# Storing the split feed-forward weights right after their split, ahead of a later weight's load

## The chip, the cores and the metric

The kernel runs on one core of a Trainium2 chip. A core has five engines with a queue of instructions each: TensorE (PE in the profile, its weight loads PEld), VectorE (DVE), ScalarE (ACT), GpSimd (POOL) and SyncE (SP), which computes nothing here and issues nearly all DMAs. Every queue is worked off in its order: an instruction that waits holds up those behind it. The metric is the device time of one execution in microseconds (us), and less is better.

## The reference

One transformer block of an encoder, in float32, over 2048 tokens of 1024 features: an RMSNorm, a projection into two kinds of attention heads, both attentions, an output projection with a residual, and then the feed-forward part, which the change concerns:

```
u2 = rms_norm(h, norm2_w[l])
gate = jnp.einsum('bsd,df->bsf', u2, w_gate[l])
up = jnp.einsum('bsd,df->bsf', u2, w_up[l])
h = h + jnp.einsum('bsf,fd->bsd', jax.nn.silu(gate) * up, w_down[l])
```

`w_gate` and `w_up` are 1024 x 2816, `w_down` is 2816 x 1024. The same weights serve all 2048 tokens.

## The kernel before

The attention part takes the first half of the execution. The feed-forward part then goes over the tokens in two halves of 1024 tokens. Within a half it goes over 11 groups of 256 hidden features (`NFG`); a group has three weight blocks of 1 MB in float32, for gate (g), up (u) and down (d).

A float32 product is done as three float16 products: every operand is split into a high part (the value rounded to float16) and a low part (what is left). In addition the 2 x 2 block products go by a scheme with seven products in place of eight (`quad` for gate and up, `down`), so each weight block is turned into seven operands of 512 columns, some of them sums and differences of quarters of the block. The seven operands in two parts are one tile `w16` of 128 x 7 x 2 x 512 float16, 1.75 MB. In the profile it is called `wg`, `wu` or `wd`.

In the first half (half 0) `load_ffn` makes this tile from the weight:

- `stage` (L829) issues the load of the block from HBM into one of two places of the tile `stages` (L826), in turn. A load can therefore only go out when the weight two places earlier has been read for the last time.
- ACT squares the block (`sq`, L869, for down L184), PE and DVE find its largest value and from it a power of two as scale (L877, L178, L195 to L199).
- `split_weight` (L207) makes the high part on ACT (L210) and the low part on DVE (L215), operand by operand. POOL makes the sums and differences in place in `stages` (L98), so the later operands wait for POOL. The last low part for the block is the last reader of its place in `stages`.
- A list `keep` takes the finished tile (L918) for a store into the HBM tensor `split`.

In the second half (half 1) nothing is split: `load_ffn` loads `split` back (L860).

The store from `keep` is not issued where it is put on the list. When `stage` has issued the load of a later weight and the list has more than one entry, it issues the oldest entry, tied behind that load by `issue_after` (L835 to L837). In the steady state that is the store of the weight two places earlier. What is left goes out after the last weight (L919 to L921).

The order of the weights is g, d, u, g, d, u and so on: the loop over the groups (L1157) begins the next group's gate in the middle of this group's gate product, this group's down weight in the middle of the down product, and the next group's up in the middle of the up product (`in_gate`, `in_down`, `in_up`, L1177 to L1191). `begin` runs the part of `load_ffn` ahead of its `yield` (load and square), `end` the rest (scale and split). The down product is done for two groups at a time, so the work repeats every two groups.

The order of each engine's queue is written when the kernel is built. A planner goes through the program with its own estimate of when each operand is ready, and puts on an engine's queue what it reckons ready, by priority, which follows the order of the program. `issue_after` adds an edge that the planner must keep. On the chip these queues are fixed, with semaphores for the operands.

Of the kernel before, what the change touches and what calls it, by code (L numbers as in the profile page):

```python
# [21 lines left out]
S, D, P = 2048, 1024, 128  # L22
NT, KT, NC = S // P, D // P, S // 512
FF = 2816
NFG = FF // 256
# [34 lines left out]
def block(tc, a, out):  # L60
    nc = tc.nc
    PE, ACT, DVE, POOL, SP = nc.tensor, nc.scalar, nc.vector, nc.gpsimd, nc.sync
    top = ExitStack()
    with top:
# [8 lines left out]
        def note(e, ns):  # L73
            load[e] += ns * KW[e]
# [34 lines left out]
        def nm(s):  # L109
            uid[0] += 1  # L110
            return f"{s}{uid[0]}"

        def c1(n=1, name="c"):
            t = cp.tile([P, n], F32, name=nm(name))
            return t
# [13 lines left out]
        def times(o, a_, b_, c=None):  # L129
            DVE.tensor_scalar(o[:], a_[:], b_[:], c, op0=ALU.mult, **({} if c is None else {"op1": ALU.mult}))  # L130
# [34 lines left out]
        split = dr.tile([NFG, 3, P, 7 * 2 * 512], F16, name="split")  # L165
# [14 lines left out]
        def scale_begin(pieces, junk=None):  # L180
            m0 = sm.tile([P, 4], F32, tag="m0", name=nm("m0"))
            for j, pc in enumerate(pieces):
                if junk is not None:
                    ACT.activation(junk, pc, AF.Square, accum_out=m0[:, j : j + 1])  # L184
                    note("A", 0.84 * int(np.prod(pc.shape[1:])) + 200)
                else:
                    DVE.tensor_reduce(m0[:, j : j + 1], pc, op=ALU.max, axis=AX.XY if len(pc.shape) > 2 else AX.X, apply_absolute_value=True)
                    note("D", 1.05 * int(np.prod(pc.shape[1:])) + 100)
            return [m0[:, j : j + 1] for j in range(len(pieces))]
# [613 lines left out]
        with ExitStack() as ph2:  # L803
# [12 lines left out]
            def pst(t):  # L816
                pst_n[0] += 1
                if pst_n[0] % 4:
                    return ps2.tile([P, 512], F32, tag="b", bufs=6, name=nm(t))
                return psj.tile([P, 512], F32, tag="pj", name=nm(t))  # L820
# [1 line left out]
            r_2, p_2, r_24 = rp2  # L822
            scales = {}

            keep, rows = [], []
            stages = fw.tile([P, 2, 2048], F32, name="stages", bufs=1)  # L826
            turn = [0]

            def stage(fg, nme):  # L829
                st = stages[:, turn[0]]  # L830
                turn[0] ^= 1
                f0 = 256 * fg
                with tc.issue_after(rows[1].ins) if (fg, nme) == (1, "u") else nullcontext():
                    d = fetch(st, f0, nme)
                if len(keep) > 1:  # L835
                    with tc.issue_after(d.ins):
                        SP.dma_start(*keep.pop(0))  # L837
                return st

            def fetch(st, f0, nme):  # L840
                if nme == "d":
                    return SP.dma_start(st.rearrange("p (f n) -> p f n", f=2), a["w_down"][0, f0 : f0 + 256, :].rearrange("(f p) n -> p f n", p=P))
                return SP.dma_start(st.rearrange("p (k n) -> p k n", k=KT), a["w_gate" if nme == "g" else "w_up"][0, :, f0 : f0 + 256].rearrange("(k p) n -> p k n", p=P))

            ones = fw.tile([P, P], BF16, name="ones", bufs=1)
            DVE.memset(ones[:], 1.0)
# [5 lines left out]
            def load_ffn(half, fg, names, W):  # L852
                eng = "ADP" if fg == 0 else WE
                sc = scales.setdefault(fg, {})
                for nme in names:
                    if half == 1:
                        yield
                        late = nme == "d" and fg == NFG - 1
                        w16 = (fd if nme == "d" and not late else fw).tile([P, 7, 2, 512], F16, tag="wd" if nme == "d" and not late else "wgu", bufs=2, name=nm("w" + nme))
                        SP.dma_start(w16[:].rearrange("p o s n -> p (o s n)"), split[fg, "gud".index(nme)])  # L860
                        W[nme] = w16
                        continue
                    st = stage(fg, nme)
                    r, p, sW = c1(), c1(), c1()
                    sq = fw.tile([P, 2048], BF16, tag="sq", bufs=1, name=nm("sq"))
                    if nme == "d":
                        cols = scale_begin([st], sq[:])
                    else:
                        ACT.activation(sq[:], st, AF.Square)  # L869
                        note("A", 1900)  # L870
                    yield
                    w16 = (fd if nme == "d" else fw).tile([P, 7, 2, 512], F16, tag="wd" if nme == "d" else "wgu", bufs=2, name=nm("w" + nme))
                    pt = pst("fsc")

                    def columns(m):
                        for k in range(KT):
                            PE.matmul(pt[:, :256], lhsT=ones[:], rhs=sq[:, 256 * k : 256 * k + 256], start=k == 0, stop=k == KT - 1)  # L877
                        DVE.tensor_reduce(m, pt[:, :256], op=ALU.max, axis=AX.X)

                    scale_end((lambda m: across(m, pt, cols)) if nme == "d" else columns, r[:], p[:], True, sW)  # L880
                    sc[nme] = (r, p, sW)
                    sW = sc[nme][2]
                    tte = "DP" if fg == 0 else "P"
                    sx = fw.tile([P, 512], F32, tag="sx", bufs=1, name=nm("sx"))

                    def put(o, src, n):
                        split_weight(w16[:, o : o + n, 0], w16[:, o : o + n, 1], src, 512 * n, sW, eng)

                    if nme == "d":
                        sv = st.rearrange("p (f h n) -> p h f n", f=2, h=2)  # L890
                        b11, b21, b12, b22 = sv[:, 0, 0], sv[:, 0, 1], sv[:, 1, 0], sv[:, 1, 1]
                        put(0, sv[:, 0], 2)
                        tt(sx[:], b22, b12, ALU.subtract, 512, tte)
                        tt(b12, b12, b11, ALU.subtract, 512, tte)
                        tt(b11, b22, b12, ALU.subtract, 512, tte)
                        tt(b21, b21, b11, ALU.subtract, 512, tte)
                        put(2, sv[:, 1], 2)
                        put(4, sv[:, 0], 2)
                        put(6, sx[:].unsqueeze(1), 1)
                    else:  # L900
                        sv = st.rearrange("p (d k f n) -> p d k f n", d=2, k=4, f=2)
                        xv = sx[:].rearrange("p (k n) -> p k n", k=4)
                        wv = w16[:].rearrange("p o s (k n) -> p o s k n", k=4)

                        def putk(o, src, n):
                            split_weight(wv[:, o : o + n, 0], wv[:, o : o + n, 1], src, 512 * n, sW, eng)

                        blk = lambda f, d: sv[:, d, :, f, :]
                        putk(0, sv[:, :, :, 0, :], 2)
                        tt(xv, blk(0, 0), blk(1, 0), ALU.subtract, 512, tte)  # L910
                        tt(blk(1, 0), blk(1, 0), blk(1, 1), ALU.add, 512, tte)
                        tt(blk(0, 0), blk(1, 0), blk(0, 0), ALU.subtract, 512, tte)
                        tt(blk(0, 1), blk(0, 1), blk(0, 0), ALU.subtract, 512, tte)
                        putk(2, sv[:, :, :, 1, :], 2)
                        putk(4, sv[:, :, :, 0, :], 2)
                        putk(6, xv.unsqueeze(1), 1)
                    W[nme] = w16
                    keep.append((split[fg, "gud".index(nme)], w16[:].rearrange("p o s n -> p (o s n)")))  # L918
                    if fg == NFG - 1 and nme == "d":  # L919
                        while keep:  # L920
                            SP.dma_start(*keep.pop(0))  # L921
                if half == 0 and "g" in names:
                    kg, F = c1(), c1()
                    times(kg, sc["g"][1], p_2, 2.0 ** -14)
                    times(F, sc["g"][0], r_2, 2.0 ** (21 - 37))
                    sc["kg"], sc["F"] = kg, F
                if half == 0 and "d" in names:
                    kd = c1()
                    times(kd, sc["u"][1], p_2)
                    times(kd, kd, sc["d"][1])  # L930
                    times(kd, kd, sc["kg"], 2.0 ** (39 - 14 - 22))
                    sc["kd"] = kd
                W.update({k: sc[k] for k in ("kg", "F", "kd") if k in sc})
# [301 lines left out]
```

## Time and profile before

| What | Value |
|---|---|
| Time, median of 3 runs | 2778.39 us (2778.34 to 2778.42) |
| The profiled execution's own time | 2775.94 us |
| Its span, first to last instruction | 2774.2 us |
| Mean granted TensorE clock | 0.964 |
| PE busy over the span | 2494.4 us (90%) |
| DVE busy | 2008.2 us (72%) |
| 33 loads of a weight block, 1 MB each | 6.5 to 6.7 us from issue to landing, in the median |
| 33 stores of a split weight, 1.75 MB each | 10.4 to 10.9 us from issue to landing, in the median |

In the profile a line such as L215 is a line of the kernel, `wg<-stages` says that a tile `wg` is written from `stages`, and `SPq` is SyncE's queue. A chain of waits is followed back from the last instruction, at each step to what released it; it names the work that set the end. The half with the split lies between about 1420 and 2155 us of the span, and its steady part repeats every 126 to 130 us.

### The profile page before, as it was taken

The numbers are of one execution on the slowest core, as the hardware profiler recorded it, in microseconds if no ns is written. First come the engines' busy times: TensorE is split into PE (matmuls) and PEld (weight loads), VectorE is DVE, ScalarE is ACT, GpSimd is POOL, SyncE is SP. The second block draws the span as 40 slices with busy tenths as digits, with TensorE's granted clock in tenths as the row PEclk, the third lists the DMA queues.
The fourth block names the chain that finished last, engine by engine and source line by source line (L and its number), as shares of the span: only waits on it lengthen the run. The fifth ranks groups of instructions, "written<-read, shape, count | busy, mean of one in ns | idle before, by whom it ended". The sixth has DMA issues, their size and how long they took to land.

```text
span 2774.2 us, 45434 instructions
## 1 busy us (share of the span) xinstructions
PE 2494.4 (90%) x17084; PEld 1409.7 (51%) x17084; DVE 2008.2 (72%) x3796; ACT 1359.0 (49%) x2539; POOL 1428.7 (52%) x1002
## 2 busy tenths in 40 slices
PE   6998989988888786888889898999899999999999
PEld 4655555555555454557775343444444444444444
DVE  6888879787989989875766877777776644444444
ACT  4665656466878878764644534343442211121120
POOL 2568767665544555546664656564645422322322
PEclk9999999999999997999999999999999999999999
DMA  7788787789999998997797565555648835535432
GB/s 228 198 165 183 145 190 162 173 172 203 198 209 195 199 181 160 191 195 208 198 309 258 199 222 200 197 203 197 231 172 284 349 141 193 205 126 205 183 121 92
DMA packets 646829, 543.52 MB, mean 196 GB/s; under 512 B 506368, under 2 KB 573952, under 8 KB 636368
## 3 DMA queue, kind: packets, MB, share of 16 engines
q1 hardware_dynamic: 644784, 538.53, 71.0%
q8 instruction: 134, 2.20, 0.3%
q0 software_dynamic: 512, 1.36, 0.2%
q10 hardware_dynamic: 1312, 0.72, 0.1%
q14 instruction: 87, 0.71, 0.1%
HBM read 261.08 MB, written 147.32 MB: 147 GB/s over the span
## 4 chain that ended last, share of the span: by engine, by line
PE 31%; DVE 9%; DMA 6%; issue 4%; ACT 3%; POOL 3%; SPq 0%; DVEq 0%; ACTq 0%; POOLq 0%
PE pd L1041 13%; PE pm L939 7%; PE pa L939 5%; PE pd L939 3%; DVE wd L215 2%; PE pe L939 2%; DMA stages<-in_w_gate_dram 2%; DMA stages<-in_w_down_dram 1%; DVE wu L215 1%; PE po L761 1%; DMA aT<-s 1%; DMA stages<-in_w_up_dram 1%; DVE cg L1006 1%; POOL s L98 1%; DVE wg L215 1%
## 5 line engine op out<-in xcount | busy, mean ns | idle before, releaser
L98 POOL TENSOR_TENSOR s<-z,s 128x1024 f16<-128x1024 f32 (+7 forms) x288 | 473.8, 1653 | 336.0 <-ACT s L89 300.0
L320 PE MATMUL pj<-w,xt 128*128 128x384 f16 x3072 | 573.9, 335 | 26.9 <-DVE st L330 11.6
L320 PEld LDWEIGHTS <-xt 128*128 128x128 f16 x3072 | 300.5, 100 | 237.6 <-issue 38.7
L1041 PE MATMUL pd<-wd,act 128*128 128x512 f16 x1764 | 395.4, 382 | 20.2 <-ACT cu L1067 16.9
L448 PE MATMUL sc<-kT,qT 128*128 128x512 f16 (+3 forms) x1280 | 347.9, 362 | 69.8 <-DVE z L558 30.9
L557 DVE TENSOR_TENSOR_SCAN z<-z,sc 128x512 f32<-128x512 f32 (+3 forms) x320 | 355.8, 1113 | 66.2 <-ACT sc L555 62.8
L458 PE MATMUL yp<-v,aT 128*128 128x64 f16 (+1 forms) x4896 | 282.5, 208 | 83.1 <-DMA aT<-s 82.2
L458 PEld LDWEIGHTS <-aT 128*128 128x128 f16 x4896 | 245.7, 102 | 174.3 <-DMA aT<-s 111.6
L939 PEld LDWEIGHTS <-wu 128*128 128x128 f16 x1848 | 182.2, 99 | 243.4 <-issue 12.8
L98 POOL TENSOR_TENSOR act<-cg,act 128x512 f16<-128x512 f32 x109 | 152.7, 1411 | 284.4 <-ACT act L1000 284.4
L939 PEld LDWEIGHTS <-wg 128*128 128x128 f16 x1848 | 181.1, 98 | 221.0 <-issue 6.4
L1041 PEld LDWEIGHTS <-act 128*128 128x128 f16 x1764 | 173.5, 98 | 232.0 <-issue 27.7
L89 ACT CAST s<-z 128x384 f16<-128x384 f32 (+7 forms) x216 | 170.4, 789 | 151.7 <-DMA aT<-s 64.2
L98 POOL TENSOR_TENSOR stages<-stages 128x512 f32<-128x512 f32 x97 | 171.6, 1770 | 129.0 <-DVE wd L215 47.0
L98 POOL TENSOR_TENSOR hs<-hs,cu 128x512 f32<-128x512 f32 x102 | 133.0, 1312 | 188.2 <-DVE cu L1047 64.6
L554 ACT ACTIVATE z<-sc,c 128x512 f32<-128x512 f32 (+3 forms) x320 | 203.1, 635 | 12.6 <-PE sc L448 10.8
L939 PE MATMUL pm<-X,wu 128*128 128x512 f16 x792 | 186.8, 390 | 18.2 <-ACT wu L210 10.8
L1000 ACT CAST act<-cg 128x512 f16<-128x512 f32 x126 | 77.7, 618 | 250.8 <-DVE cg L1006 202.7
L558 DVE TENSOR_TENSOR z<-sc,z 128x512 f32<-128x512 f32 (+3 forms) x320 | 193.6, 607 | 8.1
L555 ACT ACTIVATE sc<-sc,c 128x512 f32<-128x512 f32 (+3 forms) x320 | 195.3, 610 | 0.0
L1047 DVE SCALAR_TENSOR_TENSOR hs<-pd,c,hs 128x512 f32<-128x512 f32 x144 | 105.8, 748 | 118.4 <-PE pd L1041 110.3
L761 PE MATMUL po<-wo,mt 128*128 128x256 f16 x1536 | 180.9, 275 | 9.2 <-DVE xf L764 4.8
(245 smaller groups left out, 4140.7 us busy)
## 6 DMA issues: line engine op xcount, KB each, us to landing
xt<-xs SPq DMA_DIRECT2D x112, 512.0 KB, 4.3
hs<-hd SPq DMA_DIRECT2D x72, 512.0 KB, 4.4
hd<-hs SPq DMA_DIRECT2D x56, 512.0 KB, 5.2
split<-wg SPq DMA_DIRECT2D x11, 1792.0 KB, 10.6
split<-wu SPq DMA_DIRECT2D x11, 1792.0 KB, 10.4
split<-wd SPq DMA_DIRECT2D x11, 1792.0 KB, 10.9
wg<-split SPq DMA_DIRECT2D x11, 1792.0 KB, 7.2
wd<-split SPq DMA_DIRECT2D x11, 1792.0 KB, 9.2
```

Source lines behind the costliest of these rows:

```text
L89: ACT.copy(dst, src)
L98: (DVE if e == "D" else POOL).tensor_tensor(dst, a_, b_, op)
L320: PE.matmul(pj[:, :384], lhsT=xv[:, xi, kt, :], rhs=G["w"][:, wi, kt, :], start=n == 0, stop=n == 23)
L448: PE.matmul(sc[:, : 128 * w].rearrange("p (t n) -> p t n", n=P), lhsT=G["q"][i // 4][:, 2 - 2 * o + m, i % 4, :], rhs=G["k"][q][:, m, 0:w, ...
L458: PE.matmul(yp[:, y0 : y0 + wd], lhsT=aT[:, a_, :], rhs=v[:, v_ : v_ + wd], start=start and j == 0 and q == 0, stop=stop and j == nb - 1 a ...
L554: ACT.activation(om[:, lo:hi], sc[:, :w], AF.Sigmoid, scale=G["nkz"][:])
L555: ACT.activation(sc[:, :w], sc[:, :w], AF.Sigmoid, scale=G["kz"][:])
L557: DVE.tensor_tensor_scan(ov, ov, sc[:, :w], om[:, hi : hi + 1], op0=ALU.mult, op1=ALU.bypass)
L558: DVE.tensor_tensor(be[:, lo:hi], sc[:, :w], om[:, lo + 1 : hi + 1], ALU.mult)
L761: PE.matmul(po[:, sl], lhsT=mt[:, kt, P * xi : P * xi + P], rhs=wos[2 * h + n][wi][:, kt, :], start=q == 0, stop=q == 23)
L939: PE.matmul(ps_[:].rearrange("p (t n) -> p t n", n=P), lhsT=wv[:, wo, wi, 128 * kt : 128 * kt + 128], rhs=X[xo][:, :, xi, kt, :], start=st ...
L1041: PE.matmul(po[:], lhsT=act[:, ao, xi, 128 * j : 128 * j + 128], rhs=W["d"][:, wo, wi, :], start=start and u == 0 and q == 0, stop=u == nu ...
```

## The change

The list `keep` goes. The store of a split weight is issued in the program directly after its last operand is made, so it stands ahead of the load of the weight two places later, with no edge that ties the two. Bytes, tiles and the number of DMAs stay as they are.

```diff
-            keep, rows = [], []
+            rows = []
...
                 with tc.issue_after(rows[1].ins) if (fg, nme) == (1, "u") else nullcontext():
-                    d = fetch(st, f0, nme)
-                if len(keep) > 1:
-                    with tc.issue_after(d.ins):
-                        SP.dma_start(*keep.pop(0))
+                    fetch(st, f0, nme)
                 return st
...
                     W[nme] = w16
-                    keep.append((split[fg, "gud".index(nme)], w16[:].rearrange("p o s n -> p (o s n)")))
-                    if fg == NFG - 1 and nme == "d":
-                        while keep:
-                            SP.dma_start(*keep.pop(0))
+                    SP.dma_start(split[fg, "gud".index(nme)], w16[:].rearrange("p o s n -> p (o s n)"))
```

`fetch` only loses its return value.

More of the change, by code (lines that the diff above doesn't have):

```diff
@@ L841, in fetch @@
                 if nme == "d":
-                    return SP.dma_start(st.rearrange("p (f n) -> p f n", f=2), a["w_down"][0, f0 : f0 + 256, :].rearrange("(f p) n -> p f n", p=P))
-                return SP.dma_start(st.rearrange("p (k n) -> p k n", k=KT), a["w_gate" if nme == "g" else "w_up"][0, :, f0 : f0 + 256].rearrange("(k p) n -> p k n", p=P))
+                    SP.dma_start(st.rearrange("p (f n) -> p f n", f=2), a["w_down"][0, f0 : f0 + 256, :].rearrange("(f p) n -> p f n", p=P))
+                else:
+                    SP.dma_start(st.rearrange("p (k n) -> p k n", k=KT), a["w_gate" if nme == "g" else "w_up"][0, :, f0 : f0 + 256].rearrange("(k p) n -> p k n", p=P))
             ones = fw.tile([P, P], BF16, name="ones", bufs=1)
```

## The prediction

> **What bounds the kernel now.** I read the page first, then busy time by stretch, the chain of waits, and last SP's queue and the DMA packets around single weight loads.
>
> ```profile
> span 2774.2 us, 45434 instructions
> PE 31%; DVE 9%; DMA 6%; issue 4%; ACT 3%; POOL 3%; SPq 0%; DVEq 0%; ACTq 0%; POOLq 0%
> ```
>
> ```profile
> 1420.00:2100.00 680.00, 619.73 (x3059) 304.74 (x3057) 506.23 (x730) 294.35 (x351) 385.27 (x253) 0.97 0.61 217
> ...
> 1719.34:1845.61 126.27, 114.98 (x540) 53.21 (x540) 95.23 (x137) 52.59 (x62) 73.19 (x48) 0.98 0.58 204
> ```
>
> The columns are the stretch, its length, and busy time of PE, PEld, DVE, ACT and POOL, then the granted clock and the DMA share. While weights are split (1420 to 2100 us), TensorE is idle for 680.0 - 619.7 = 60 us. One pair of feature groups (1719 to 1846 us) has 11 us of that. So the stage is near TensorE's own limit, but it is not at it. The chain says what holds it:
>
> ```profile
> by line: PE pd L1041 18.3%; issue 9.2%; DVE wd L215 8.1%; DMA stages<-in_w_gate_dram 6.2%; DMA stages<-in_w_down_dram 5.8%; DVE wu L215 5.5%; PE pm L939 4.2%; DMA stages<-in_w_up_dram 3.9%; PE pa L939 3.8%; DVE cg L1006 3.2%; DVE wg L215 2.
> ```
>
> These are shares of 1420 to 2100. Gate loads have 6.2% of 680 = 42 us, down loads 39 us, up loads 27 us: 108 us of the path that sets the end is time in which a 1 MB load flies. One load is 6.4 to 6.7 us on that chain (below), so this is 16 loads: 6 gate, 6 down, 4 up. The pieces of the chain in one pair, in order of time (start, length, what):
>
> ```profile
> 1775.15 2.10 DVE wd L215
> 1777.28 6.60 DMA stages<-in_w_gate_dram
> 1786.38 1.06 ACT wu L210
> 1794.05 2.36 DVE wu L215
> 1796.43 6.44 DMA stages<-in_w_down_dram
> 1802.95 2.00 ACT sq L184 x2
> 1804.96 1.06 ACT wg L210
> 1807.36 6.66 DMA stages<-in_w_up_dram
> 1816.52 1.06 ACT wd L210
> 1828.36 2.10 DVE wd L215
> 1830.48 6.71 DMA stages<-in_w_gate_dram
> 1845.61 0.58 PE pd L1041
> ```
>
> The last low part of a weight (DVE, L215) frees its place in `stages`; the load of the weight two places later goes out 0.02 to 0.03 us later; ACT squares it, and only behind that square does ACT go on with the split of the weight between them. Four loads are on the path in this pair before the down product starts.
>
> **What the change does at one load.** It adds no byte and no DMA, and takes the `keep` edge away. Today SP issues the load, and behind it the store:
>
> ```profile
> 1777.28 0.38 SPq L843 DMA_DIRECT2D stages<-in_w_gate_dram  x1
> 1777.71 0.57 SPq L837 DMA_DIRECT2D split<-wd  x1
> ```
>
> Both are ready at the same moment: the load waits for the last reader of the place in `stages`, which is the same DVE instruction that finishes the tile to be stored (1775.15 + 2.10 = 1777.25). After the change the store is earlier in the program, so with equal readiness the planner puts it first. Nothing new is then waited for on SP: what is queued behind (the loads and stores of `hs`) stood behind the load's wait for the same instruction. The price is in the DMA queue.
>
> ```profile
> GB/s 0 0 0 0 0 0 0 0 0 0 0 0 0 0 0 0 0 27 96 96 68 96 96 137 191 137 96 177 177 164 164 218 150 205 246 232 259 273 246 287
> DMA packets 281, 0.29 MB, mean 96 GB/s; under 512 B 0, under 2 KB 281, under 8 KB 281
> ...
> DMA packets 512, 0.52 MB, mean 262 GB/s; under 512 B 0, under 2 KB 512, under 8 KB 512
> ...
> DMA packets 101, 1.22 MB, mean 210 GB/s; under 512 B 16, under 2 KB 16, under 8 KB 16
> ```
>
> These are the packets of 1777 to 1780, 1780 to 1782 and 1784.2 to 1790. Until 1782 all 793 packets are the load's small ones, though the store was issued at 1777.71. Once the load has landed (1777.28 + 6.60 = 1783.88), what is left is 1.22 MB in 85 large packets and 16 tiny ones. So the two transfers of SP's queue do not share the DMA engines; the first one issued goes first. Today the load pays nothing for the store. Turned round, it waits for it:
>
> ```profile
> split<-wd SPq DMA_DIRECT2D x1, 1792.0 KB, 10.4
> stages<-in_w_gate_dram SPq DMA_DIRECT2D x1, 1024.0 KB, 6.6
> ```
>
> The pair is done at 0.43 + 10.4 = 10.8 us after the load's issue, and the load at 6.6. With the store first the pair should be done in the same 10.8 us, and the load is now its last part: 10.8 - 6.6 = 4.2 us later. The 0.6 us that SP takes to issue the store lies under the store's own transfer. The bounds: in 1777 to 1780 the first 17 of 40 slices carry nothing, so 1.0 us passes between issue and first byte; if that and the slow slices after it come to lie under the store's end, the price is 4.2 - 1.0 = 3.2. If the load only starts when a store has landed, a store that goes out with nothing ahead of it tells:
>
> ```profile
> split<-wu SPq DMA_DIRECT2D x1, 1792.0 KB, 6.6
> ```
>
> 6.6 us, and then the load's 6.6 - 1.0 = 5.6 of transfer: 12.2 - 6.6 = 5.6 us. There is one place today where a load meets the rest of a store of the load before it:
>
> ```profile
> 1558.56 0.57 SPq L837 DMA_DIRECT2D split<-wg  x1
> 1567.35 0.38 SPq L843 DMA_DIRECT2D stages<-in_w_gate_dram  x1
> ...
> split<-wg SPq DMA_DIRECT2D x1, 1792.0 KB, 10.5
> ...
> stages<-in_w_gate_dram SPq DMA_DIRECT2D x1, 1024.0 KB, 8.7
> ```
>
> The store had 1558.56 + 10.5 - 1567.35 = 1.7 us to go, and the load took 8.7 instead of 6.6, 2.1 more. That speaks for the full price and none hidden; I take 4.2 and keep 3.2 to 5.6.
>
> The Trainium skill, in "DMA: Bandwidth & Descriptors", section "Two DMAs through the same engine are not ordered", says that within one queue of an engine descriptors start in order but are pipelined, reads and writes being separate. By that rule the load's first reads would run under the store's last writes and a load would lose about 3.2 us; in the forecast below this would make 42 us of 55. The 8.7 us row is against it, and I go by the row.
>
> **The sum.** Of 33 loads 31 have a store beside them, but only the ones on the path count: those off it have slack that this trace does not price, and a pushed load on the path moves all that follows. If every queue kept its order, that is 16 x 4.2 = 67 us. But the planner writes the queues anew with its own estimate of the landings, and could put ACT's waiting pieces ahead of the squares. What they look like now:
>
> ```profile
> 1783.22 0.14 DVE L199 TENSOR_SCALAR c<-c 128x1 f32<-128x1 f32 x1
> 1810.71 0.15 DVE L199 TENSOR_SCALAR c<-c 128x1 f32<-128x1 f32 x1
> ...
> 1814.10 1.91 ACT L869 ACTIVATE sq<-stages 128x2048 bf16<-128x2048 f32 x1 [5.45 <-DMA stages<-in_w_up_dram]
> ```
>
> ```profile
>   DMA stages<-in_w_up_dram: 55.8, 8
> ...
>   DMA stages<-in_w_gate_dram: 13.2, 5
>   DMA stages<-in_w_down_dram: 6.9, 5
> ```
>
> At an up load the split of the down weight is ready at 1810.9 (its scale is made by L199), and ACT sits for 5.45 us in front of the square until 1814.1. The planner must have reckoned with a landing some 3 us or more ahead of the real one there; so a landing moved by 4.2 leaves that order likely as it is. The second list (what ended ACT's idle time ahead of instructions on `stages`, 1590 to 2100 us) has it at 7.0 us for each of 8 up loads, 2.6 for gate and 1.4 for down. I let the 4 up loads and the 6 gate loads on the path keep their order. For the 6 down loads, where ACT hardly waits and a swap takes little, I take half. 13 x 4.2 = 55 us.
>
> No part pays this back. Earlier stores would free a `w16` tile earlier, but nothing waits for one: the splits on ACT wait for POOL and for the scale, in no row for a store.
>
> ```profile
> L210 ACT ACTIVATE wg<-stages,c 128x1024 f16<-128x1024 f32 x24 | 26.6, 1141 | 14.9 <-POOL stages L98 12.5 <-DVE c L199 2.4
> ```
>
> The other half only reads `split`, long after. So its span goes from 2774.2 to 2829; the median shown is 4.2 us above that span (2778.4), and comes to 2833 us.
>
> **The rivals.**
>
> *All the order is kept.* 16 loads at 4.2 make 67 us: 2846, and at 5.6 each 90 us, 2868. For it: ACT's waits above show a planner that is off by more than the shift. Against it: any change makes it write all queues of this stage anew.
>
> *The planner gives way, and it gets faster.* If it counts the store into the landing, it puts the pending splits ahead of the squares at most of the 16 places. Then the loads leave the path, and what TensorE waits for behind them today shrinks:
>
> ```profile
> PE pm L939 <- ACT wu L210: 10.8, 4, 2.9
> PE fsc L877 <- ACT sq L869: 7.1, 4, 2.1
> PE pm L939 <- DVE wu L215: 6.3, 4, 1.8
> ```
>
> That is 24 us in four pairs (1590 to 2100). Half of it gone is 12 us: 2766. It decides from the point where fewer than about 3 of the 16 loads stay on the path (3 x 4.2 = 13, against the 12). For it: a ready split that stands 5 us behind a square is a poor order that a later landing could undo. Against it: the split's POOL steps and the down product still need each weight before TensorE goes on, and each still comes 4.2 us later.
>
> *It does not do what it says.* The load is ready as the store is; if the planner takes the load first, as now, SP's queue is today's and the time 2778. Against it: the store is ahead in the program, and has no more to wait for.
>
> *Most is absorbed.* 2 to 6 of 16 places kept, without gain: 8 to 25 us, 2787 to 2804.
>
> **How the numbers follow.** Forecast, 7 to 14 places or a price down to 3.2, 2804 to 2842 us: 0.45. All kept, above 2842: 0.17, a fifth of it above 2860. Absorbed: 0.13. As now, within 0.2% (5.5 us; that is about what a measurement of this kernel can tell from no change): 0.10. Faster: 0.15. Slower is 0.45 + 0.17 + 0.13 = 0.75. The range leaves out the top of the all-kept case (0.05) and the lower part of the faster one (0.10): 2770 to 2858. The likeliest case's own is 2804 to 2842.
>
> **What would show it.** In SP's queue `split<-w` stands ahead of `stages<-in_w` at the same freed place. The loads land some 10.8 us after the DVE instruction that frees the place, the stores in 6 to 7 after their issue. ACT's waits for landings grow by up to 4.2 us for each load, TensorE's idle time between 1420 and the end of the split by about 55, and the half without splits keeps its length. The forecast is wrong if loads land as early as now, if the load stays ahead of the store, or if ACT's squares stand behind splits that they now precede.

## The result: 2756 us, faster by 0.75%

| Kernel | Median | Ratio to before, 95% interval |
|---|---|---|
| before | 2778.36 us | |
| changed | 2756.14 us (2754.26 to 2761.84) | 0.9925 (0.9908 to 0.9942) |

The change saves 22 us, where the prediction had it cost 55. It ends on the side of the second rival (the planner gives way, 2766), with more gain than that rival had.

The page of the changed kernel, its span and the chain by engine and by line:

```profile
span 2752.2 us, 45466 instructions
PE 32%; DVE 8%; DMA 6%; POOL 4%; issue 4%; ACT 3%; SPq 0%; POOLq 0%; DVEq 0%; ACTq 0%
```

The chain between 1420 and 2100 us:

```profile
by line: PE pd L1036 18.2%; issue 7.6%; DVE wd L215 7.1%; DMA stages<-in_w_down_dram 5.4%; PE pa L934 5.2%; POOL stages L98 4.6%; PE pm L934 4.6%; DVE cg L1001 3.8%; DVE wu L215 3.5%; DMA stages<-in_w_up_dram 3.4%; DVE cg L98 3.2%; ACT wu L
```

Down loads still have 5.4% of 680 = 37 us of the path and up loads 23 us. Gate loads, the largest with 42 us before, have fallen out of the list; one of 9.3 us is left. In all, 7 loads with 69 us stand on the chain, where there were 16 with 108.

Four pairs of groups, 1588 to 2078 us (stretch, length, busy time of PE, PEld, DVE, ACT and POOL, clock, DMA share, GB/s):

```profile
1588.01:1711.00 122.99, 114.50 (x537) 53.08 (x537) 94.54 (x137) 52.49 (x62) 72.87 (x48) 0.99 0.63 219
1711.00:1832.38 121.38, 113.12 (x537) 52.60 (x537) 95.42 (x137) 52.48 (x62) 72.87 (x48) 0.99 0.61 209
...
sum 489.57, PE 460.55 PEld 213.35 DVE 377.87 ACT 210.16 POOL 290.00; mean PE 115.14 PEld 53.34 DVE 94.47 ACT 52.54 POOL 72.50
```

The same four pairs before, 1590.57 to 2100.91:

```profile
sum 510.34, PE 467.57 PEld 214.53 DVE 381.26 ACT 210.63 POOL 292.66; mean PE 116.89 PEld 53.63 DVE 95.32 ACT 52.66 POOL 73.16
```

A pair takes 122.4 us, against 127.6 before. Of the 20.8 us, TensorE's idle time gives 42.8 - 29.0 = 13.8. The other 7.0 are matmuls that ran at a granted clock of 0.95 to 1.00 instead of 0.95 to 0.98. Why the clock was higher is not shown, so a third of the gain in these pairs is not explained by the waits.

The swap on SP is there. SP's queue and the packets at the gate load of the pair that the prediction followed (stretches 1768.5 to 1774.3, 1774.3 to 1775.4):

```profile
1768.57 0.32 SPq L916 DMA_DIRECT2D split<-wd  x1
1768.95 0.43 SPq L841 DMA_DIRECT2D stages<-in_w_gate_dram  x1
...
GB/s 0 0 0 0 0 0 1483 99 0 494 1088 0 0 0 791 791 0 0 1088 494 0 0 1384 198 0 593 989 0 0 791 791 0 0 0 395 494 395 297 0 0
DMA packets 128, 1.84 MB, mean 316 GB/s; under 512 B 0, under 2 KB 0, under 8 KB 0
...
split<-wd SPq DMA_DIRECT2D x1, 1792.0 KB, 6.8
stages<-in_w_gate_dram SPq DMA_DIRECT2D x1, 1024.0 KB, 9.4
...
GB/s 0 0 0 0 0 0 37 37 37 112 75 112 186 112 186 186 149 261 224 186 298 298 224 410 484 149 559 410 223 521 410 261 521 261 410 447 261 484 447 261
DMA packets 264, 0.25 MB, mean 231 GB/s; under 512 B 16, under 2 KB 264, under 8 KB 264
```

All 128 large packets of the store go first, then the small ones of the load. From the store's issue to the load's landing it is 0.38 + 9.4 = 9.8 us; the load alone took 6.6. So this load lands 3.2 us later. A down load with nothing else beside it lands 0.4 + 8.8 = 9.2 us after the store's issue, where it took 6.5: 2.7 us later. Some loads lose more, such as an up load (issued at 1734.44) that took 12.3 us with transfers of `hs` around it in SP's queue.

What changed beside it stands on ACT. The gate load's place in the two kernels, before first:

```profile
1783.96 1.91 ACT L869 ACTIVATE sq<-stages 128x2048 bf16<-128x2048 f32 x1 [2.95 <-DMA stages<-in_w_gate_dram]
...
1786.29 2.19 ACT L210 ACTIVATE wu<-stages,c 128x1024 f16<-128x1024 f32 x2
1788.38 0.71 ACT L210 ACTIVATE wu<-sx,c 128x512 f16<-128x512 f32 x1
```

```profile
1775.14 2.18 ACT L210 ACTIVATE wu<-stages,c 128x1024 f16<-128x1024 f32 x2
1777.23 0.70 ACT L210 ACTIVATE wu<-sx,c 128x512 f16<-128x512 f32 x1
...
1778.41 1.90 ACT L867 ACTIVATE sq<-stages 128x2048 bf16<-128x2048 f32 x1
1781.64 1.15 ACT L210 ACTIVATE wu<-stages,c 128x1024 f16<-128x1024 f32 x1 [1.33 <-POOL stages L98]
```

Before, ACT waited 2.95 us for the gate load to square it and only then made the high parts of up. After, three of up's four high parts stand ahead of the square. The load lands later, and ACT no longer waits for it. The same holds at the up load, where the ready split had waited 5.45 us for the square:

```profile
1802.31 2.19 ACT L210 ACTIVATE wd<-stages,c 128x1024 f16<-128x1024 f32 x2 [0.60 <-DVE c L199]
1804.41 0.71 ACT L210 ACTIVATE wd<-sx,c 128x512 f16<-128x512 f32 x1
...
1807.81 1.91 ACT L867 ACTIVATE sq<-stages 128x2048 bf16<-128x2048 f32 x1 [2.19 <-DMA stages<-in_w_up_dram]
```

In the steady part the planner moved the square at both gate loads of a pair (at one from no high part ahead to three, at the other from three to four) and at one of its two up loads, the one that was on the path; it left it at both down loads. TensorE's waits, 1587 to 2078 us:

```profile
PE pd L1036 <- ACT cu L1062: 15.2, 4, 5.2
PE fsc L875 <- ACT sq L867: 12.0, 7, 3.2
PE fsc L177 <- ACT sq L184: 5.4, 3, 3.0
PE pd L1036 <- DVE cg L963: 0.6, 1, 0.6
```

The 10.8 and 6.3 us that TensorE waited for the split of up are gone. The waits for squares have grown from 7.1 to 17.4 (12.0 + 5.4).

### The profile page after: what moved, and what is told of

It reads as the page before. It is cut to its first block, busy times and chain, and to the rows that moved or that the text cites. A ratio compares the mean times of both kernels' runs of the same rounds, so it can differ in the third digit from the quotient of the medians.

```text
span 2752.2 us, 45466 instructions
## 1 busy us (share of the span) xinstructions
PE 2482.9 (90%) x17084; PEld 1404.8 (51%) x17084; DVE 2005.2 (73%) x3796; ACT 1357.3 (49%) x2539; POOL 1428.8 (52%) x1002
## 4 chain that ended last, share of the span: by engine, by line
PE 32%; DVE 8%; DMA 6%; POOL 4%; issue 4%; ACT 3%; SPq 0%; POOLq 0%; DVEq 0%; ACTq 0%
PE pd L1036 13%; PE pm L934 7%; PE pa L934 5%; PE pd L934 3%; PE pe L934 2%; DVE wd L215 2%; DMA aT<-s 2%; DMA stages<-in_w_down_dram 1%; POOL stages L98 1%; POOL s L98 1%; PE po L761 1%; DVE cg L1001 1%; DVE cg L98 1%; DVE wu L215 1%; DMA stages<-in_w_up_dram 1%
## 5 line engine op out<-in xcount | busy, mean ns | idle before, releaser
L448 PE MATMUL sc<-kT,qT 128*128 128x512 f16 (+3 forms) x1280 | 348.3, 363 | 67.1 <-DVE z L558 31.0
L934 PE MATMUL pm<-X,wu 128*128 128x512 f16 x792 | 178.9, 379 | 0.0
```

The lines of the kernel that those rows point to most:

```text
L448: PE.matmul(sc[:, : 128 * w].rearrange("p (t n) -> p t n", n=P), lhsT=G["q"][i // 4][:, 2 - 2 * o + m, i % 4, :], rhs=G["k"][q][:, m, 0:w, ...
L934: PE.matmul(ps_[:].rearrange("p (t n) -> p t n", n=P), lhsT=wv[:, wo, wi, 128 * kt : 128 * kt + 128], rhs=X[xo][:, :, xi, kt, :], start=st ...
```

## The experiments

The theory after the result (A): the swap in itself costs a later landing at each load on the path, as the prediction said, and the gain comes from ACT's new order, which the planner wrote because it reckoned with the later landing. The rivals: (B) the stores' earlier place gains; (C) any change writes the queues anew and the time falls where it may; and later (D) the swap costs next to nothing.

**The tie alone taken away.** The store stays where it was in the program, behind the load.

```diff
                 if len(keep) > 1:
-                    with tc.issue_after(d.ins):
-                        SP.dma_start(*keep.pop(0))
+                    SP.dma_start(*keep.pop(0))
```

> The kernel before without the tie of the store behind the load; in the program the store stays behind the load. SP's queue in the steady part and the order of squares and splits on ACT stay those of before; a few other places change. Theory A (the gain comes from ACT's new order: squares behind the pieces of the split that is under way): 2778, within 6 us. Theory B (the gain comes from the stores' place in SP's queue): 2778 as well. Theory C (the gain comes from the queues being written anew, whatever the change): any time, 10 to 20 us away from 2778 is as likely as 2778.

Measured: 2784.29 us, ratio 1.0029 (1.0017 to 1.0041). In the steady part ACT's order of squares and splits is that of before, and the time is 7 to 8 us above it, just outside the 6 us that A and B allowed. This rewriting of some places of the queues was worth 0.3%, and it went the other way. It sets no bound for another rewriting, so C is not excluded by it.

**Load first, ACT's new order.** Edges between each square, from the seventh weight on, and the four high parts of the weight before it give the order that ACT has in the changed kernel. All else is left to the planner.

```diff
+            def queued(later, earlier):
+                tc.add_manual_dep(later.ins, earlier.ins.name, <order of issue only>)
+
+            def square(ins):                  # called with the square of weight k
+                k = len(squares); squares.append(ins)
...                                            # nothing more for the first six weights
+                n = AHEAD_OF_SQ[k - 1]        # 0, 3 or 4, read off the changed kernel's trace
+                for j, z in enumerate(<the four high parts of weight k - 1>):
+                    queued(*((ins, z) if j < n else (z, ins)))
```

> The kernel before (load first, store tied behind) with edges that give ACT, from the seventh weight on, the order of squares and split pieces of the changed kernel. Theory A: at least the gain of the change, 2756, and up to 7 loads on the chain of the changed kernel x 3.1 us (9.75 us from the freed place to the landing against 6.65) = 22 us more, so 2734 to 2756. Theory B: the gain is gone, 2778. Theory C: no relation, 2755 to 2790.

Measured: 2751.4 us, ratio 0.99 (0.9879 to 0.9921). The gain is there without the swap, so B fails. That it is a little larger than with the swap is not settled: the two intervals overlap.

**Store first, ACT's old order.** The same edges on the changed kernel, with the counts read off the trace of before.

> The changed kernel (store first) with edges that give ACT the order of squares and split pieces of the kernel before. Theory A: slower than before by the later landing at the 16 loads of the chain, 16 x 3.1 = 50 us: 2828; at least 2800. Theory B: the time of the changed kernel, 2756, within 10. Theory C: no relation, 2755 to 2790.

Measured: 2780.46 us, ratio 1.0015 (1.0004 to 1.0026). The gain is gone, as A has it, but the loss of 50 us did not come. The chain between 1420 and 2100 us:

```profile
by line: DMA stages<-in_w_gate_dram 8.7%; issue 8.2%; PE pa L958 7.1%; PE pm L958 7.0%; PE pd L1060 6.4%; DMA stages<-in_w_up_dram 6.2%; POOL stages L98 6.2%; DVE wd L218 5.7%; DMA stages<-in_w_down_dram 5.6%; DVE wg L218 3.9%; PE pd L958 3
```

Loads have 20.5% of 680 = 139 us of this path, 31 more than before, and the span is only 4 us longer. So the later landing is on the path and something else gave 27 us back. The edges had fixed ACT's squares and nothing else; the planner had written the other queues anew. That called for a kernel in which they are held as well.

**Every queue held.** Both kernels trace the same instructions on TensorE, VectorE, ScalarE and GpSimd, in the same program order. So the queue of one kernel can be laid on the other: from the first place where the two differ to the end, each instruction is tied behind the one that the other kernel has in front of it. SP's queue is left to the program.

```diff
+def pin(tc, PE, ACT, DVE, POOL):
+    traced = list(tc.nc.cur_bb.bb.instructions)
+    for e, eng in (("PE", PE), ("ACT", ACT), ("DVE", DVE), ("POOL", POOL)):
+        mine = [i for i in traced if i.engine == eng.engine and <an instruction>]
+        order = [mine[k] for k in <places read off the other kernel's built queue>]
+        for x, y in zip(order, order[1:]):
+            tc.add_manual_dep(y, x.name, <order of issue only>)
```

Store first, with the queues of before:

> The changed kernel's SP order (store first) while the queues of TensorE, VectorE, ScalarE and GpSimd are held, by edges from each instruction to the next in the feed-forward part, exactly to the order of the kernel before. This is the case in which every queue keeps its order. Theory A (a later landing is paid at each load of the old chain, and only the new order pays it back): 16 loads x 2.7 to 3.1 us = 43 to 50 us over before, about 2822 to 2828. Rival D (the swap costs little in itself, as the 3 us of store first with ACT's old order suggest): 2778 to 2785. Rival B (the stores' place is what gains): 2756.

Measured: 2832.68 us, ratio 1.0202 (1.0174 to 1.023). Its span, the chain between 1420 and 2150 us, and what ended ACT's idle time ahead of instructions on `stages` (1590 to 2150):

```profile
span 2820.5 us, 45456 instructions
```

```profile
by line: PE pd L1036 18.4%; DMA stages<-in_w_gate_dram 7.8%; issue 7.6%; DVE wd L215 6.9%; DMA stages<-in_w_up_dram 6.4%; DMA stages<-in_w_down_dram 6.3%; PE pm L934 4.7%; PE pa L934 4.6%; DVE wu L215 4.3%; DVE cg L1001 2.8%; DVE wg L215 2.
...
  DMA stages<-in_w_up_dram: 84.5, 8
  DMA stages<-in_w_gate_dram: 33.7, 7
  DMA stages<-in_w_down_dram: 22.3, 5
```

20.5% of 730 = 150 us of loads on the chain. The chain piece by piece has 16 loads again (6 gate, 5 up, 5 down), 9.4 us each; 150 - 108 = 42 us more. SP issues the load 0.4 us later as well, which is 6 us over 16. Together 48, and the span grew by 46.3. ACT waits for landings 140 us in these 560, where it waited 76 in 510. So the swap costs 16 times the later landing when nothing gives way: this half of A is shown, and B and D fail. The median grew by some 56 us (48 to 64 by the interval), more than the 50 that A allowed, and the profiled execution by less. The four executions took the longer the lower their mean granted clock was: 2822 us at 0.961, 2828 at 0.957, 2838 and 2839 at 0.954. So the rest seems to go with the clock, and why the clock fell is open.

This kernel and the one above it, 2780 us, have the same order of the store and the load and the same squares on ACT in the steady part. They differ in the other places of the compute queues, which the planner was free to write there, and by some 52 us. So those places matter as much as the squares do, and which of them gave the time back is not shown. To that extent C holds.

Load first, with the queues of the changed kernel:

> The SP order of the kernel before (load first, store tied behind) while the queues of TensorE, VectorE, ScalarE and GpSimd are held to the order of the changed kernel. Theory A: the whole gain of the new order without the later landings: 7 loads stand on the chain of the changed kernel, so up to 22 us below 2756: 2734 to 2751. Rival D: 2751 to 2756. Rival B: 2778.

Measured: 2745.72 us, ratio 0.9894 (0.9875 to 0.9912). The chain between 1420 and 2100 us:

```profile
by line: PE pd L1041 22.4%; DVE wd L215 8.1%; issue 7.7%; POOL stages L98 6.2%; PE pm L939 5.7%; PE pa L939 5.7%; DVE cg L1006 4.7%; DVE cg L98 4.0%; ACT wu L210 2.7%; DVE wu L215 2.6%; PE po L761 2.3%; DVE wg L215 2.0%; ACT wg L210 1.9%; A
```

No load is left on the chain, to its end. In the four pairs TensorE waits 3.8 us for squares (1590 to 2080), against 17.4 in the changed kernel with the same queues; that difference goes with the later landing. At one place ahead of the held part ACT's queue is not that of the changed kernel: a gate square at 1469 us stands in front of the split. The four corners, by the ratio to before, as us on 2778:

| | load first | store first |
|---|---|---|
| queues of before | 0 | +56 |
| queues of the changed kernel | -29 | -21 |

The new queues gain 29 us with the load first. With the store first they turn 56 lost into 21 gained. The swap itself costs 56 us with the old queues. With the new ones it costs some 9, and there the two intervals touch; 7 loads on the chain at 3.1 us would allow up to 22.

**Which loads.** Load first, with ACT's new order at the gate loads only, and at the up loads only (the counts of before elsewhere).

> The kernel before with ACT's order of the changed kernel at the gate loads only (three or four pieces of the up split ahead of the gate's square), and of before at the others. Theory A: most of the gain of the same edges at all weights if TensorE's waits for the split of up (17 us over four pairs in the trace of before) are what they take away: 2755 to 2765. If it is the up loads (7 us wait of ACT at each) that matter: 2772 to 2778. Theory B: 2778.

Measured: 2774.78 us, ratio 0.9989 (0.9976 to 1.0001). The first expectation, most of the gain from the gate loads, is missed; it is the second case.

> The kernel before with ACT's order of the changed kernel at the up loads only (three pieces of the down split ahead of up's square), and of before at the gate and down loads. The same at the gate loads gave 3 us, at all loads 26. If the two add: 2778 - 23 = 2755. If both are needed at once, since either wait holds the same chain: 2770 to 2778.

Measured: 2763.61 us, ratio 0.9955 (0.9938 to 0.9971). Gate alone gives 3 us, which its interval does not tell from nothing; up alone 12, between the two cases that were expected; both (with two down places) 28. So they seem to do more together than the sum, though the intervals leave room for the plain sum. With the gates alone four up, six down and two gate loads are still on the chain (1420 to 2160), and ACT still waits for the up loads:

```profile
  DMA stages<-in_w_up_dram: 64.5, 8
  DMA stages<-in_w_down_dram: 4.6, 4
```

That is ACT's idle time in the gate-only kernel, 1588 to 2080. The 13.2 us for gate are gone, the up loads' 55.8 have become 64.5. With the up loads alone it is four gate loads of the steady part that stay on the chain.

**Did the planner move the squares because of the landing, or because of the store's place in the program?** The list `keep` stays, and the store stays at the later load, but the tie is turned round.

```diff
+                s = SP.dma_start(*keep.pop(0)) if len(keep) > 1 else None
                 with tc.issue_after(rows[1].ins) if (fg, nme) == (1, "u") else nullcontext():
-                    d = fetch(st, f0, nme)
-                if len(keep) > 1:
-                    with tc.issue_after(d.ins):
-                        SP.dma_start(*keep.pop(0))
+                    with tc.issue_after(s.ins) if s is not None else nullcontext():
+                        fetch(st, f0, nme)
```

> The kernel before with the list kept and the store's place in the program kept (at the later load), but the tie turned round: the load is tied behind the store. If the planner rewrites the queues because it reckons with a later landing of the loads (Theory A with a planner that counts the store), it writes ACT's order of the changed kernel here too: 2756, within 6. If the earlier place of the store in the program is what did it, the queues stay those of before and the time is that of store first with old queues: 2833, at least 2810.

Measured: 2759.38 us, ratio 0.9923 (0.9908 to 0.9938). In the steady part ACT has the squares of the changed kernel; at an up load, for example, three of down's high parts run from 1809.2 to 1812.0 and the square starts at 1814.7. So it is the order of the two DMAs from which the planner made the new queues, not the place of the store in the program. That it does so through its estimate of the landing fits, and is not shown step by step.

**A version that beats both.** Load first, with every square behind all four, or behind three, of the high parts of the weight before it.

> The kernel before (load first) with every square, from the seventh weight on, behind all four high pieces of the weight before it, down loads too. If a square ahead of a ready piece only costs: 2751 (edges for the changed kernel's order) or below, down to 2740. If a square that waits for the last piece, which waits for GpSimd, makes the scale of the next weight late: above 2751, up to 2775.

Measured: 2748.67 us, ratio 0.9899 (0.9881 to 0.9917).

> The kernel before (load first) with every square, from the seventh weight on, behind three of the four high pieces of the weight before it. Behind all four gave 2749, behind the changed kernel's mix of none, three and four 2751. If only a square that stands ahead of ready pieces costs: 2745 to 2752. If the down squares have to go first so that down's scale is ready in time: 2752 to 2765.

Measured: 2745.11 us, ratio 0.9877 (0.9859 to 0.9896). With three high parts ahead everywhere the kernel is 1.2% faster than before and has the lowest ratio of all, though its interval overlaps those of the other load-first kernels at 2746 to 2751 us; a square behind the fourth part gives no more. Its span and its chain between 1420 and 2100 us:

```profile
span 2740.9 us, 45446 instructions
...
by line: PE pd L1065 23.3%; DVE wd L218 9.0%; issue 6.8%; PE pm L963 5.9%; PE pa L963 5.8%; POOL stages L98 4.4%; DVE cg L1030 4.3%; DVE cg L98 3.6%; DMA stages<-in_w_down_dram 2.9%; DVE wu L218 2.7%; PE pd L963 2.0%; ACT wu L213 2.0%; PE p
```

One kind of load is left on it, with 2.9% of 680 = 20 us. So with the load first a better order of ACT's squares gives the whole gain. That ACT's squares alone give it is not shown: in every kernel with edges on the squares the planner wrote the rest anew, and no run moves the squares with the other queues held.

## Why the prediction was wrong

- *What bounds the stage* held: 16 loads on the chain, in front of which ACT stands with the split of the weight between. The kernel with all queues held, store first, has 16 on its chain too.
- *The store goes ahead of the load, in the same queue, and the load waits for it* held: 128 large packets, then the small ones. SP's waits for the last reader now stand ahead of the store. Its waits ahead of loads of `hs`, for `hd<-hs` to land, grew from 70 to 88 us (1590 to 2100 before, 1588 to 2078 after); whether that cost time is not shown.
- *The price of 4.2 us at a load* was too high: 3.1 to 3.2 at gate and up loads with nothing else beside them, 2.7 at such down loads, and 3.0 in the mean over the 16 loads of the kernel with all queues held ((150 - 108 + 6) / 16). The prediction took the 8.7 us row, one load that met the last 1.7 us of a store, as proof that nothing hides. The packets around that load (1567.3 to 1569.3) do not bear this out: its small packets begin about 1.1 us after its issue, some 0.7 us before the store has landed. So its setup was hidden too, and where the 2.1 us went is not settled. In the changed kernel the load's bytes follow 0.5 us after the store's last packet (two empty slices of 0.15 us and six of 0.03 us in the rows above), where a load alone needs 1.0 us from its issue. The lower price, 3.2, is the one that the prediction set beside the Trainium skill's rule ("DMA: Bandwidth & Descriptors", section "Two DMAs through the same engine are not ordered": descriptors start in order but are pipelined). The trace agrees with the rule: the load's first bytes come at 1774.5, before the store lands at 1768.57 + 6.8 = 1775.4.
- *The sum if every queue keeps its order*: 16 loads, 67 us. With the right price it is 48 to 50, and the kernel built for just that case measured 46 in its profiled execution and 56 in the median. The mechanism was right there.
- *The 4 up loads and the 6 gate loads on the path keep their order; half of the down loads give way.* This is the step that failed. It came out the other way round: gate and up gave way in each pair, down stayed, and 7 loads were left on the path instead of 13. The argument was that the planner had reckoned with an up landing 3 us or more ahead of the real one, so that another 4.2 would change nothing. But those 3 us say how far the planner was off from the chip, not how far its choice lay from turning, and that can't be read from the chip's waits. For the gate loads no reason was given, though the row shown there has the split's scale ready at 1783.4, only 0.5 us ahead of the landing. Turning the order of the two DMAs was enough, as the kernel with the tie turned round shows.
- *No part pays this back* followed from that step and fell with it. The second rival had the mechanism and the sign, but only half of TensorE's 24 us behind the splits, 12 us. It let the kernel get faster only with fewer than about 3 loads left on the path; 7 stayed, and it got faster all the same. The new queues are worth 29 with the load first and, after the later landings, 21 to 22.
- *What would prove it wrong* named the case that came: ACT's squares behind the splits that they had preceded.
- A slip in the chances bears on nothing: 14 places at 4.2 end at 2837, where the forecast's upper end is given as 2842.

## What to carry to other kernels

When a planner writes the queues, an edit of one DMA's place is also an edit of every queue that waits for it: price the fixed order, and then look for in-order waits that stand ahead of ready work, because those are what the rewritten queue took away here. Where a trace shows an engine waiting for a landing with ready work behind that wait, move that wait back first; here a kernel with such edges gained 1.2%, with the order of the DMAs left as it was. To tell the two apart, hold every compute queue to the other kernel's order and change the DMAs alone.

## What the runs showed that was not expected

A load and a store in one queue are done sooner with the store first: 9.8 us from the first issue to the last landing, against 10.8 with the load first. This fits a setup of the load that lies mostly under the store's packets, 0.5 us of gap where the load alone has 1.0. A kernel with the same instructions and only some queue places written differently (the tie taken away) moved by 0.29%, clear of its interval, so a difference of that size after an edit need not be the edit's own. And the granted clock of the split stage went with its waits: 0.93 to 0.95 in three pairs of the kernel with all queues held and the store first (1652.14 to 2067.80), 0.96 to 0.97 in the same pairs before (1650.19 to 2032.40). Their matmuls took 361.0 us against 348.3, so 12.7 of the 33.5 us by which these pairs grew are longer matmuls. Why the clock does so is not shown.
